# Opening of a decoder-layer kernel: c spread by a VectorE shuffle, squares of four tiles summed on TensorE, the shifted row also kept in float32, and the second block's weights fetched in halves

## The chip, the cores and the metric

The kernel runs on one NeuronCore of a Trainium2 chip. The metric is the device time of one launch in microseconds, as the median of several runs. Engines are named as in the profile: PE is TensorE, DVE is VectorE, ACT is ScalarE, POOL is GpSimd, SP is SyncE, which here only issues DMAs. PEld is PE's loading of weights.

## What is computed

One layer on 256 tokens of width 1024, all in float32: a SwiGLU feed-forward block, a mixer with two branches, and a second SwiGLU block, each behind an RMS norm whose result is scaled and shifted by columns that are computed from a conditioning vector c, and a final norm. The change touches only the beginning of the first SwiGLU block:

```python
c_act = jax.nn.silu(c)
mod = c_act @ ada_w[l] + ada_b[l]
sh1, sc1, g1, sh2, sc2, g2, sh3, sc3, g3 = jnp.split(mod, N_MOD, axis=-1)
u = modulate(rms_norm(h, norm_ffn1_w[l]), sh1, sc1)      # u = normed * (1 + sc1) + sh1
h = h + FFN_RESIDUAL_WEIGHT * g1[:, None, :] * swiglu(u, ffn1_w_in[l], ffn1_w_out[l])
```

## The kernel before

Activations lie transposed: 8 tiles of 128 features by 256 tokens. A float32 product is made of three passes in a faster format (fp32r): each operand is split into a high part (a cast on ACT) and a low part (a subtraction on DVE), and PE multiplies high by high, high by low and low by high.

The opening runs over the eight feature tiles; I call the work of one tile a block and count from 0. For block `kt` the kernel needs a column of the scale (`sc1`), a column of the shift (`sh1`), the normed tile, and 128 rows of `ffn1_w_in` in two parts of 1024 columns (gate and up). Each column is a dot product of 1024 elements in every partition: DVE multiplies 128 rows of `ada_w` (a tile `ada`, its first half for the scale and its second for the shift) by `cb`, the vector silu(c) spread over all partitions, and sums along the row (`ada_dots`, L196). Then:

- ACT makes `am`, the scale with the norm's weight (L416); DVE multiplies the input tile by it and by the reciprocal root of the mean square (`normed`, L425), which gives `xn`.
- ACT makes the shift column `modc` (L420) and then `uh`, the high part of `xn` plus shift (`u_high`, L429). DVE makes `ul`, the low part, from `xn`, the shift and `uh` (`u_low`, L432).
- ACT casts the two halves of the weights to their high parts (`highs`, L410) and DVE makes the low parts (`lows`, L413). Both write to tiles named `wh`.
- PE runs 48 matmuls of 128x256 (`first_mms`, L441): 16 tiles (8 of gate, 8 of up), first high by `uh`, then high by `ul`, then low by `uh`. In the last block the tiles are sorted by pairs, gate and up in turn.

In the opening PE, ACT, DVE and SP work through their instructions in the order in which the code is written (`manual_schedule`): an instruction that waits holds up all that stand behind it on its engine. In the loop over the blocks the code of block `kt + 1` for DVE and ACT stands ahead of the matmuls of block `kt`.

Before block 0, c has to be spread and the statistics made. c is loaded as one row (`crow`, one partition) and spread by two matmuls with a row of ones (L388) into PSUM, from which ACT takes its Silu into `cb` (L185). The tiles of the input come with the identity matrix and a few columns in one tensor, `head`, whose first half is issued on ACT's queue and whose second on SP's. Of each half, ACT squares two tiles and DVE two (L392, L394); DVE adds them (L395, and L397 for the last), and PE sums over partitions by matmuls against a matrix of 1/1024 (`mean1`, L400) into `stat`. ACT takes the root (`r`), DVE the reciprocal, PE spreads it over the partitions (L457), and a few matmuls of ones by ones (`warm`, L377) fill gaps.

All weights are packed by the host in the order in which they are fetched, and `fetch` (L118) issues each as one DMA on SP's queue. For block 0 the gate and up halves are two transfers of 512 KB, for the other blocks one of 1 MB; the scale and shift rows of each block are two of 512 KB. Completions are counted by eight semaphores used in turn, so a DMA is issued only when the one eight before it has landed.

Of the kernel before, what the change touches and what calls it, by code (L numbers as in the profile page):

```python
# [82 lines left out]
def layer(ctx: ExitStack, tc: tile.TileContext, a, out, packing):  # L83
# [14 lines left out]
    def nm(s):  # L98
        uid[0] += 1
        return f"{s}_{uid[0]}"  # L100
# [66 lines left out]
    triu = k[:, K_TRI:K_TRI + P]  # L167
    mean_m = k[:, K_M:K_M + P]
    ones = cst.tile([P, P], F32, name="ones")
    dve.memset(ones, 1.0)  # L170
    epsc = cst.tile([P, 1], F32, name="epsc")
    dve.memset(epsc, EPS)

    phase = {"load": None, "uses": []}

# [178 lines left out]
    with (tc.tile_pool(name="ep", bufs=1) as ep,  # L354
          tc.manual_schedule(engines={e.engine for e in (pe, act, dve, nc.sync)})):
        table("silu_and_others")
        crow = ep.tile([1, D], F32, name="crow")
        nc.sync.dma_start(crow, a["c"])
        for queue, c0, c1 in ((act, 0, 4 * T), (nc.sync, 4 * T, N_HEAD)):
            queue.dma_start(head[:, c0:c1], a["head"][:, c0:c1])  # L360

        def ada01(kt):
            st = ep.tile([P, 2 * D], F32, tag="ada", name=nm("ada"), bufs=4)
            return [ada_rows(st[:, i * D:(i + 1) * D], 1 - i, kt) for i in range(2)]

        def w01(kt):
            st = stage()
            parts = ((0,), (1,)) if kt == 0 else ((0, 1),)
            for js in parts:
                fetch(st[:, js[0] * F1 * P:(js[-1] + 1) * F1 * P], w1, lambda m, js=js: np.stack(  # L370
                    [m[kt * P:(kt + 1) * P, j * FFN:j * FFN + F1 * P] for j in js], axis=1))
            return st.rearrange("p (j n) -> p j n", j=2)

        def warm(n):
            ps = misc_ps()
            for i in range(n):
                pe.matmul(ps[:, :P], ones, ones, start=True, stop=True)  # L377

        sts, wst = [], []
        for kt in range(3):  # L380
            sts.append(ada01(kt))
            wst.append(w01(kt))
# [3 lines left out]
        cps, stat = [misc_ps() for _ in range(2)], misc_ps()  # L386
        for q in range(2):
            pe.matmul(cps[q], ones[0:1, :], crow[:, q * 512:(q + 1) * 512], start=True, stop=True)  # L388
        for i in range(2):
            f0 = 4 * i  # L390
            sq = ep.tile([P, 4, T], F32, tag="sq2", name=nm("sq2"), bufs=2)
            act.activation(sq[:, 0:2, :], h[:, f0:f0 + 2, :], AF.Square)  # L392
            lookup(cb[:, i * 512:(i + 1) * 512], cps[i], AF.Silu)
            dve.tensor_tensor(sq[:, 2:4, :], h[:, f0 + 2:f0 + 4, :], h[:, f0 + 2:f0 + 4, :], ALU.mult)  # L394
            dve.tensor_tensor(sq[:, 0:2, :], sq[:, 0:2, :], sq[:, 2:4, :], ALU.add)  # L395
            if i == 1:
                dve.tensor_tensor(sq[:, 0, :], sq[:, 0, :], sq[:, 1, :], ALU.add)  # L397
            for f in range(2 - i):
                for tt in range(2):
                    pe.matmul(stat[:, tt * P:(tt + 1) * P], sq[:, f, tt * P:(tt + 1) * P], mean1,  # L400
                              start=i == f == tt == 0, stop=i == tt == 1, skip_group_check=True)
        warm(1)
        u = new_u()
        am = sp.tile([P, KD], F32, tag="am", name=nm("am"), bufs=2)

# [21 lines left out]

        def u_high(kt, xn):
            act.activation(u[0][:, kt, :], xn, AF.Identity, bias=modc[:, 0, kt:kt + 1])  # L429

        def u_low(kt, xn):
            dve.scalar_tensor_tensor(u[1][:, kt, :], xn, modc[:, 0, kt:kt + 1],  # L432
                                     u[0][:, kt, :].bitcast(F32), ALU.add, ALU.subtract)

        def first_mms(kt, hw):
            tiles = [(j, f) for j in range(2) for f in range(F1)]
# [2 lines left out]
            for w, x in ((0, 0), (0, 1), (1, 0)):  # L439
                for j, f in tiles:  # L440
# [4 lines left out]
        ada_dots(sts[0][0], 1, 0)  # L445
        dve.scalar_tensor_tensor(bn1, head[:, H_AB + KD:H_AB + 2 * KD], 1.0,
                                 head[:, H_N1:H_N1 + KD], ALU.add, ALU.mult)
        r = ep.tile([P, 2], F32, name="r2")
        table("sqrt_and_others")
        lookup(r, stat[:, 0:T:P], AF.Sqrt, bias=epsc)  # L450
# [8 lines left out]
        warm(3)  # L459
        ada_dots(sts[0][1], 0, 0)  # L460
        xn = normed(0, ps[:, :T])
        shift_col1(0)
# [9 lines left out]
        banks += [[misc_ps().rearrange("p (f t) -> p f t", f=2) for _ in range(2)] for _ in range(2)]  # L472
        for kt in range(KD):
            if kt + 3 < KD:
                sts.append(ada01(kt + 3))
                wst.append(w01(kt + 3))
            if kt + 1 < KD:
                hw_next = halves(kt + 1)
                ada_dots(sts[kt + 1][0], 1, kt + 1)
                scale_col1(kt + 1)  # L480
                highs(kt + 1, hw_next, 0)
                ada_dots(sts[kt + 1][1], 0, kt + 1)
                xn = normed(kt + 1, rb)
                shift_col1(kt + 1)
                u_high(kt + 1, xn)
                highs(kt + 1, hw_next, 1)
                lows(kt + 1, hw_next, 0)
                u_low(kt + 1, xn)
                lows(kt + 1, hw_next, 1)
            first_mms(kt, hw)  # L490
            hw = hw_next
# [626 lines left out]
```

## Time and profile before

| what | value |
|---|---|
| median of 3 runs | 821.73 us (821.46 to 821.89) |
| the profiled execution | 821.32 us |
| its span, from the first to the last instruction | 819.3 us |
| mean granted clock of TensorE | 0.998 |
| first matmul of block 0 (L441) | 11.92 us after the span's start |
| DMA in the first 20 us | 366 GB/s on average |

A row of the timeline gives the start in us from the span's start, the duration, the engine, the line, the operation, what it writes and reads, the shape, how many were merged (x4), and in brackets how long the engine had been idle before and what ended that. Instructions on one engine overlap a little, so the next one's start tells more of the cost than the duration. A row with SPq or ACTq is the issue of a DMA, not the transfer. Matmuls in plain float32 show up as two passes.

### The profile page before, as it was taken

Reading aid. Unit: us, or ns where it says so; the run is one execution under the profiler, and the core shown is the slowest. Engines: PE = TensorE matmul, PEld = TensorE weight load, DVE = VectorE, ACT = ScalarE, POOL = GpSimd, SP = SyncE. Lnnn points to the kernel's source line nnn. Section 1 sums busy time; section 2 is a strip of 40 time slices with the busy share of each in tenths; the row PEclk is TensorE's granted clock in tenths of the full one; section 3 lists DMA queues with packets and bytes.
Section 4 is the critical chain, followed back from the end, with each engine's and each line's share of the span. In section 5 each row is a group of like instructions: output and inputs, shape, how many; then the busy total and the mean of one; then the engine's idle time right before and its main releaser. Section 6 shows DMA issues by size and latency. Waiting matters only on the chain.

```text
span 819.3 us, 15834 instructions
## 1 busy us (share of the span) xinstructions
PE 808.9 (99%) x6580; PEld 782.6 (96%) x6580; DVE 677.3 (83%) x1003; ACT 505.6 (62%) x722; POOL 16.2 (2%) x31
## 2 busy tenths in 40 slices
PE   8999999999999999999999999999999999999997
PEld 6999999999999989999999999999999999999886
DVE  7989899977989889788898778977988987665693
ACT  6565445555898678766465569765658754545342
POOL 0000000000200010000000000000000001100000
PEclk9999999999999999999999999999999999999999
DMA  9999889854695556546658664554565589785521
GB/s 366 414 418 350 312 350 363 341 200 155 233 318 188 202 173 225 189 148 212 239 192 310 231 232 154 206 207 154 193 224 183 198 316 261 277 289 183 194 103 51
DMA packets 31161, 195.69 MB, mean 239 GB/s; under 512 B 3681, under 2 KB 4321, under 8 KB 10482
## 3 DMA queue, kind: packets, MB, share of 16 engines
q1 hardware_dynamic: 28370, 186.07, 62.9%
q0 software_dynamic: 2432, 7.90, 3.1%
q8 instruction: 51, 0.84, 0.4%
q10 hardware_dynamic: 288, 0.72, 0.3%
q14 instruction: 20, 0.16, 0.1%
HBM read 192.54 MB, written 2.13 MB: 238 GB/s over the span
## 4 chain that ended last, share of the span: by engine, by line
PE 93%; DVE 3%; ACT 2%; DMA 1%; issue 0%; SPq 0%; ACTq 0%
PE proj L151 25%; PE proj L153 25%; PE proj L152 25%; PE proj L147 2%; PE proj L148 2%; PE proj L441 2%; PE proj L149 2%; PE misc L441 2%; DMA wst<-in_ffn_w_in_dram 1%; PE misc L746 1%; DVE wh L138 1%; PE misc L890 1%; PE misc L222 1%; PE misc L756 1%; ACT s L185 0%
## 5 line engine op out<-in xcount | busy, mean ns | idle before, releaser
L138 DVE TENSOR_TENSOR wh<-wst,wh 128x1024 fp32r<-128x1024 f32 (+1 forms) x262 | 315.9, 1212 | 85.6 <-ACT wh L137 85.1
L137 ACT CAST wh<-wst 128x1024 fp32r<-128x1024 f32 (+1 forms) x262 | 272.0, 1043 | 164.9 <-PE proj L153 125.0
L151 PE MATMUL proj<-uh,wh 128*128 128x256 f32 (+1 forms) x1096 | 304.0, 277 | 0.0
L152 PE MATMUL proj<-ul,wh 128*128 128x256 f32 (+1 forms) x1096 | 303.1, 277 | 0.0
L153 PE MATMUL proj<-uh,wh 128*128 128x256 f32 (+1 forms) x1096 | 303.0, 276 | 0.0
L153 PEld LDWEIGHTS proj<-uh,wh 128*128 128x128 f32 x1096 | 205.8, 188 | 0.2 <-issue 0.2
L152 PEld LDWEIGHTS proj<-ul,wh 128*128 128x128 f32 x1096 | 205.8, 188 | 0.1
L151 PEld LDWEIGHTS proj<-uh,wh 128*128 128x128 f32 x1096 | 205.8, 188 | 0.1
L151 PE MATMUL proj<-s,wh 128*128 128x256 f32 x312 | 86.7, 278 | 0.2 <-ACT s L142 0.2
L153 PE MATMUL proj<-s,wh 128*128 128x256 f32 x312 | 86.3, 277 | 0.0
L152 PE MATMUL proj<-s,wh 128*128 128x256 f32 x312 | 86.2, 276 | 0.0
L151 PEld LDWEIGHTS proj<-s,wh 128*128 128x128 f32 x312 | 58.5, 188 | 0.4 <-ACT s L142 0.4
L153 PEld LDWEIGHTS proj<-s,wh 128*128 128x128 f32 x312 | 58.6, 188 | 0.0
L152 PEld LDWEIGHTS proj<-s,wh 128*128 128x128 f32 x312 | 58.6, 188 | 0.0
L196 DVE SCALAR_TENSOR_TENSOR ada<-ada,cb 128x1024 f32<-128x1024 f32 x48 | 57.2, 1217 | 0.0
L147 PE MATMUL proj<-uh,wh 128*128 128x256 f32 x152 | 42.0, 276 | 0.0
L148 PE MATMUL proj<-uh,wh 128*128 128x256 f32 x152 | 42.0, 276 | 0.0
L149 PE MATMUL proj<-ul,wh 128*128 128x256 f32 x152 | 42.0, 276 | 0.0
L151 PE MATMUL proj<-ah,wh 128*128 128x256 f32 x152 | 42.0, 276 | 0.0
L152 PE MATMUL proj<-al,wh 128*128 128x256 f32 x152 | 42.0, 276 | 0.0
L153 PE MATMUL proj<-ah,wh 128*128 128x256 f32 x152 | 42.0, 276 | 0.0
L185 ACT ACTIVATE s<-proj 128x512 f32<-128x512 f32 x33 | 19.7, 597 | 35.5 <-PE proj L153 33.4
(271 smaller groups left out, 1371.3 us busy)
## 6 DMA issues: line engine op xcount, KB each, us to landing
wst<-in_mix_w_in_dram SPq DMA_DIRECT2D x52, 1024.0 KB, 4.9
wst<-in_ffn_w_in_dram SPq DMA_DIRECT2D x43, 1024.0 KB, 6.3
wst<-in_ffn_w_out_dram SPq DMA_DIRECT2D x18, 1024.0 KB, 5.0
ada<-in_ada_w_dram SPq DMA_DIRECT2D x16, 1024.0 KB, 8.3
wst<-in_ada_w_dram SPq DMA_DIRECT2D x12, 1024.0 KB, 5.0
ada<-in_ada_w_dram SPq DMA_DIRECT2D x16, 512.0 KB, 12.8
wst<-in_w_br_ssd_dram SPq DMA_DIRECT2D x8, 1024.0 KB, 4.9
wst<-in_w_br_ret_dram SPq DMA_DIRECT2D x8, 1024.0 KB, 4.9
```

The costliest lines, as they stand in the source:

```text
L137: act.copy(hi, v)
L138: dve.tensor_tensor(lo, v, hi.bitcast(F32), ALU.subtract)
L147: pe.matmul(o, l[1], r[0], start=False, stop=False, skip_group_check=skip)
L148: pe.matmul(o, l[0], r[0], start=False, stop=False, skip_group_check=skip)
L149: pe.matmul(o, l[0], r[1], start=False, stop=False, skip_group_check=skip)
L151: pe.matmul(o, l[0], r[0], start=first, stop=False, skip_group_check=skip)
L152: pe.matmul(o, l[0], r[1], start=False, stop=False, skip_group_check=skip)
L153: pe.matmul(o, l[1], r[0], start=False, stop=last, skip_group_check=skip)
L185: phase["uses"].append(act.activation(*args, **kw).ins)
L196: dve.scalar_tensor_tensor(st[:, i, :], st[:, i, :], 1.0, cb, ALU.mult, ALU.mult, accum_out=raw[:, j, f0 + i:f0 + i + 1])
L222: pe.matmul(ps[:, :T], mean, s, start=i == 0, stop=i == len(parts) - 1)
L441: pe.matmul(banks[f // 2][j][:, f % 2, :], hw[w][j][:, f * P:(f + 1) * P], u[x][:, kt, :], start=kt == w == x == f % 2 == 0, stop=kt == KD ...
```

## The change

The constants `ones` and `epsc` are set later. `crow` becomes a tile of 128 partitions that DVE sets to zero; one DMA then writes c into partitions 0, 32, 64 and 96, and a shuffle on DVE copies the first partition of each group of 32 to the whole group, into `cb`. The DMA of c stands behind SP's half of `head` in place of ahead of it, and waits for the zeroing. The Silu is one instruction on `cb` in place of two from PSUM. The matmuls that spread c go; ten matmuls of ones stand in their place, and the other two groups grow from 1 to 2 and from 3 to 5.

For the second half of `head` DVE doesn't add any more: PE sums four squared tiles in place of one.

`u_high` gets a second activation that writes `xn` plus shift, in float32, back to `xn`; `u_low` then subtracts `uh` from it without the shift.

The weights of block 1 are fetched as two halves, in the order scale rows, gate half, shift rows, up half. `block` replaces `ada01` and `w01`; the other blocks' order stays. `bn1` is made ahead of the first dot product.

```diff
-        crow = ep.tile([1, D], F32, name="crow")
-        nc.sync.dma_start(crow, a["c"])
+        crow = ep.tile([P, D], F32, name="crow")
+        dve.memset(crow, 0.0)
+        dve.memset(ones, 1.0)
+        dve.memset(epsc, EPS)
         for queue, c0, c1 in ((act, 0, 4 * T), (nc.sync, 4 * T, N_HEAD)):
             queue.dma_start(head[:, c0:c1], a["head"][:, c0:c1])
+        nc.sync.dma_start(crow[0:P:32, :], a["c"].broadcast_to([4, D]))
...
+            scale = rows(0)
+            if kt == 1:
+                cols(0)
+            shift = rows(1)
+            for js in ((0,), (1,)) if kt == 0 else ((1,),) if kt == 1 else ((0, 1),):
+                cols(*js)
...
-        for q in range(2):
-            pe.matmul(cps[q], ones[0:1, :], crow[:, q * 512:(q + 1) * 512], start=True, stop=True)
+        dve.stream_shuffle(cb, crow, [0] * 32)
+        stat = misc_ps()
+        warm(10)
         for i in range(2):
             f0 = 4 * i
             sq = ep.tile([P, 4, T], F32, tag="sq2", name=nm("sq2"), bufs=2)
             act.activation(sq[:, 0:2, :], h[:, f0:f0 + 2, :], AF.Square)
-            lookup(cb[:, i * 512:(i + 1) * 512], cps[i], AF.Silu)
+            if i == 0:
+                lookup(cb, cb, AF.Silu)
             dve.tensor_tensor(sq[:, 2:4, :], h[:, f0 + 2:f0 + 4, :], h[:, f0 + 2:f0 + 4, :], ALU.mult)
-            dve.tensor_tensor(sq[:, 0:2, :], sq[:, 0:2, :], sq[:, 2:4, :], ALU.add)
-            if i == 1:
-                dve.tensor_tensor(sq[:, 0, :], sq[:, 0, :], sq[:, 1, :], ALU.add)
-            for f in range(2 - i):
+            if i == 0:
+                dve.tensor_tensor(sq[:, 0:2, :], sq[:, 0:2, :], sq[:, 2:4, :], ALU.add)
+            for f in (2, 3, 0, 1) if i else (0, 1):
...
         def u_high(kt, xn):
             act.activation(u[0][:, kt, :], xn, AF.Identity, bias=modc[:, 0, kt:kt + 1])
+            act.activation(xn, xn, AF.Identity, bias=modc[:, 0, kt:kt + 1])

         def u_low(kt, xn):
-            dve.scalar_tensor_tensor(u[1][:, kt, :], xn, modc[:, 0, kt:kt + 1],
-                                     u[0][:, kt, :].bitcast(F32), ALU.add, ALU.subtract)
+            dve.tensor_tensor(u[1][:, kt, :], xn, u[0][:, kt, :].bitcast(F32), ALU.subtract)
```

The order of instructions, first ACT's in one block of the loop (block 1). Before:

```order
L416 ACTIVATE am_143<-raw,bn_116,head 128x1
L410 CAST wh_186<-wst_107 128x1024
L420 ACTIVATE modc<-raw,head 128x1
L429 ACTIVATE uh_141<-xn_192,modc 128x256
L410 CAST wh_187<-wst_107 128x1024
```

After:

```order
L424 ACTIVATE am_157<-raw,bn_118,head 128x1
L418 CAST wh_203<-wst_106 128x1024
L428 ACTIVATE modc<-raw,head 128x1
L437 ACTIVATE uh_155<-xn_209,modc 128x256
L438 ACTIVATE xn_209<-xn_209,modc 128x256
L418 CAST wh_204<-wst_106 128x1024
```

The new activation (L438) stands between `uh` and the second CAST, in each of the eight blocks.

Next DVE's from its start to the reciprocal. Before:

```order
L170 MEMSET ones 128x128
L172 MEMSET epsc 128x1
L384 MEMSET mean_114 128x128
L394 TENSOR_TENSOR sq_10_122<-head 128x512
L395 TENSOR_TENSOR sq_10_122<-sq_10_122 128x512
L394 TENSOR_TENSOR sq_11_131<-head 128x512
L395 TENSOR_TENSOR sq_11_131<-sq_11_131 128x512
L397 TENSOR_TENSOR sq_11_131<-sq_11_131 128x256
L196 SCALAR_TENSOR_TENSOR ada_98,raw<-ada_98,cb 128x1024
L446 SCALAR_TENSOR_TENSOR bn_116<-head 128x8
L454 RECIPROCAL r_146<-r_146 128x2
```

After:

```order
L356 MEMSET crow 128x1024
L357 MEMSET ones 128x128
L358 MEMSET epsc 128x1
L391 MEMSET mean_116 128x128
L393 STREAM_SHUFFLE cb<-crow 128x1024
L402 TENSOR_TENSOR sq_9_132<-head 128x512
L404 TENSOR_TENSOR sq_9_132<-sq_9_132 128x512
L402 TENSOR_TENSOR sq_10_141<-head 128x512
L453 SCALAR_TENSOR_TENSOR bn_118<-head 128x8
L194 SCALAR_TENSOR_TENSOR ada_99,raw<-ada_99,cb 128x1024
L462 RECIPROCAL r_160<-r_160 128x2
```

The shuffle, which waits for the transfer of c, stands ahead of all squares; two adds are gone.

Last SP's first transfers. Before:

```order
L358 DMA crow<-in_c_dram 1x1024
L360 DMA head<-in_head_dram 128x1176
L118 DMA ada_98<-in_ada_w_dram 128x1024 x2
L118 DMA wst_101<-in_ffn_w_in_dram 128x1024 x2
L118 DMA ada_104<-in_ada_w_dram 128x1024 x2
L118 DMA wst_107<-in_ffn_w_in_dram 128x2048
```

After:

```order
L360 DMA head<-in_head_dram 128x1176
L361 DMA crow<-in_c_dram 4x1024
L118 DMA ada_99<-in_ada_w_dram 128x1024 x2
L118 DMA wst_100<-in_ffn_w_in_dram 128x1024 x2
L118 DMA ada_105<-in_ada_w_dram 128x1024
L118 DMA wst_106<-in_ffn_w_in_dram 128x1024
L118 DMA ada_105<-in_ada_w_dram 128x1024
L118 DMA wst_106<-in_ffn_w_in_dram 128x1024
```

c comes second, and block 1's weights (`wst_106`) are two transfers with the shift rows between them.

More of the change, by code (lines that the diff above doesn't have):

```diff
@@ L169, in layer @@
     ones = cst.tile([P, P], F32, name="ones")
-    dve.memset(ones, 1.0)
     epsc = cst.tile([P, 1], F32, name="epsc")
-    dve.memset(epsc, EPS)
     phase = {"load": None, "uses": []}
@@ L356, in layer, with block, rows, cols @@
         table("silu_and_others")
-        crow = ep.tile([1, D], F32, name="crow")
-        nc.sync.dma_start(crow, a["c"])
+        crow = ep.tile([P, D], F32, name="crow")
+        dve.memset(crow, 0.0)
+        dve.memset(ones, 1.0)
+        dve.memset(epsc, EPS)
         for queue, c0, c1 in ((act, 0, 4 * T), (nc.sync, 4 * T, N_HEAD)):
             queue.dma_start(head[:, c0:c1], a["head"][:, c0:c1])
[L362 to L370, printed above, removed]
-                    [m[kt * P:(kt + 1) * P, j * FFN:j * FFN + F1 * P] for j in js], axis=1))
-            return st.rearrange("p (j n) -> p j n", j=2)
+        nc.sync.dma_start(crow[0:P:32, :], a["c"].broadcast_to([4, D]))
+        sts, wst = [], []
+        def block(kt):
+            ada, w = ep.tile([P, 2 * D], F32, tag="ada", name=nm("ada"), bufs=4), stage()
+            def rows(i):
+                return ada_rows(ada[:, i * D:(i + 1) * D], 1 - i, kt)
+            def cols(*js):
+                fetch(w[:, js[0] * F1 * P:(js[-1] + 1) * F1 * P], w1, lambda m: np.stack(
+                    [m[kt * P:(kt + 1) * P, j * FFN:j * FFN + F1 * P] for j in js], axis=1))
+            scale = rows(0)
[4 more added lines that the diff above has]
+                cols(*js)
+            sts.append((scale, shift))
+            wst.append(w.rearrange("p (j n) -> p j n", j=2))
         def warm(n):
@@ L377, in warm @@
                 pe.matmul(ps[:, :P], ones, ones, start=True, stop=True)
-        sts, wst = [], []
         for kt in range(3):
-            sts.append(ada01(kt))
-            wst.append(w01(kt))
+            block(kt)
         mean1 = ep.tile([P, P], F32, name="mean1")
@@ L392, in layer @@
             act.activation(sq[:, 0:2, :], h[:, f0:f0 + 2, :], AF.Square)
[L393 removed]
+            if i == 0:
+                lookup(cb, cb, AF.Silu)
             dve.tensor_tensor(sq[:, 2:4, :], h[:, f0 + 2:f0 + 4, :], h[:, f0 + 2:f0 + 4, :], ALU.mult)
[L395 to L398 removed]
+            if i == 0:
+                dve.tensor_tensor(sq[:, 0:2, :], sq[:, 0:2, :], sq[:, 2:4, :], ALU.add)
+            for f in (2, 3, 0, 1) if i else (0, 1):
                 for tt in range(2):
                     pe.matmul(stat[:, tt * P:(tt + 1) * P], sq[:, f, tt * P:(tt + 1) * P], mean1,
[L401 to L402 removed]
+                              start=i == f == tt == 0, stop=i == f == tt == 1,
+                              skip_group_check=True)
+        warm(2)
         u = new_u()
@@ L458, in layer @@
                       start=True, stop=True)
-        warm(3)
+        warm(5)
         ada_dots(sts[0][1], 0, 0)
@@ L474, in layer @@
             if kt + 3 < KD:
-                sts.append(ada01(kt + 3))
-                wst.append(w01(kt + 3))
+                block(kt + 3)
             if kt + 1 < KD:
```

3 lines of the change are left out of this document (1 added, 2 removed).

## The prediction

> **What bounds the kernel now.** I read the page first: busy time by engine, then the chain of work that ended last.
>
> ```profile
> PE 808.9 (99%) x6580; PEld 782.6 (96%) x6580; DVE 677.3 (83%) x1003; ACT 505.6 (62%) x722; POOL 16.2 (2%) x31
> PE 93%; DVE 3%; ACT 2%; DMA 1%; issue 0%; SPq 0%; ACTq 0%
> ```
>
> PE is busy for 808.9 of 819.3 us and carries 93% of the chain. What the change can win or lose is therefore PE time that is empty, or that it makes empty, in the opening: the eight blocks of L441, 48 matmuls each. Next the chain in order of time, from the span's start:
>
> ```profile
> 4.85 11.54 DMA wst<-in_ffn_w_in_dram
> 16.40 0.40 ACT wh L410
> ...
> 17.68 0.52 ACT uh L429
> 18.24 0.74 PE proj L441 x4
> ```
>
> Block 1's first matmul, at 18.24, hangs on one 1 MB transfer, issued at 4.85 and in use at 16.40. This is the gap that the split fetch is aimed at. From 18.24 on PE has no gap in the opening. The timeline of a later block (block 5), ACT's rows and then DVE's, says why that is a near thing:
>
> ```profile
> 38.18 0.39 ACT L416 ACTIVATE am<-raw,bn,head 128x1 f32<-128x1 f32 x1 [2.44 <-DVE ada L196]
> 38.47 1.04 ACT L410 CAST wh<-wst 128x1024 fp32r<-128x1024 f32 x1
> 39.41 0.28 ACT L420 ACTIVATE modc<-raw,head 128x1 f32<-128x1 f32 x1
> 39.78 0.51 ACT L429 ACTIVATE uh<-xn,modc 128x256 fp32r<-128x256 f32 x1
> 40.20 1.03 ACT L410 CAST wh<-wst 128x1024 fp32r<-128x1024 f32 x1
> ```
>
> ```profile
> 36.91 1.22 DVE L196 SCALAR_TENSOR_TENSOR ada<-ada,cb 128x1024 f32<-128x1024 f32 x1
> ...
> 39.20 0.48 DVE L425 SCALAR_TENSOR_TENSOR xn<-head,am,rb 128x256 f32<-128x256 f32 x1
> 39.60 1.22 DVE L413 TENSOR_TENSOR wh<-wst,wh 128x1024 fp32r<-128x1024 f32 x1
> 40.74 0.48 DVE L432 SCALAR_TENSOR_TENSOR ul<-xn,modc,uh 128x256 fp32r<-128x256 f32 x1
> 41.26 1.23 DVE L413 TENSOR_TENSOR wh<-wst,wh 128x1024 fp32r<-128x1024 f32 x1
> 42.41 1.22 DVE L196 SCALAR_TENSOR_TENSOR ada<-ada,cb 128x1024 f32<-128x1024 f32 x1
> ```
>
> Follow it as a loop between two engines (ACT above, DVE below). DVE makes the dot product with the scale rows (36.91); ACT waits for it, idle for 2.44 us, then does am, the first CAST, the shift column, uh and the second CAST, which ends at 40.20 + 1.03 = 41.23. DVE's second `wh` subtraction starts at 41.26, 0.03 later, though DVE itself was ready sooner: a 128x256 operation lets the next one start 0.40 after it (39.20, 39.60), here at 40.74 + 0.40 = 41.14. The dot product of the next block follows at 42.41. One turn takes 42.41 - 36.91 = 5.50 us and runs **through ACT's second CAST**. PE's turn is hardly longer: from block 1's first matmul at 18.24 to block 7's at 52.05 are six blocks, 5.64 us each.
>
> ```profile
> 52.05 1.18 PE L441 MATMUL proj<-uh,wh 128*128 128x256 f32 x8
> 51.18 1.04 ACT L410 CAST wh<-wst 128x1024 fp32r<-128x1024 f32 x1
> ```
>
> In block 7 the matmuls are sorted so that the third needs the second CAST. That CAST ends at 51.18 + 1.04 = 52.22; PE reaches its third matmul at 52.05 + 2 x 0.12 = 52.29. The slack is 0.07 us.
>
> **The shifted row in float32: the term that decides.** The new `xn` activation (128x256, Identity with a bias) is queued on ACT between uh and the second CAST, so it lies in the loop in every block, eight times. Its form is that of L429. Lower bound: from uh to the next instruction are 40.20 - 39.78 = 0.42 us, as for any instruction that needn't wait. Upper bound: the new one waits on ACT's own semaphore (it overwrites xn, which uh reads), and an instruction that waits so starts 0.09 late: the shift column ends at 39.41 + 0.28 = 39.69 and uh, which reads it, starts at 39.78. That makes 0.51 + 0.09 = 0.60. I take 0.51 us, the row's own duration.
>
> A turn becomes 5.50 + 0.51 = 6.01 us, over PE's 5.64, so PE waits for ACT in each block. Eight of them push the end of the last opening CAST by 8 x 0.51 = **+4.1 us** (3.4 to 4.8). What DVE may save by a plainer `ul` counts nothing: it stands ahead of an instruction that waits for the CAST.
>
> **The second block's weights.** Two waits in the same loop go. Block 1's first CAST stood still until 16.40; by the 0.29 us from am to CAST in block 5 it could have started at 15.24 + 0.29 = 15.53. Block 3's stood 27.52 - 27.05 - 0.29 = 0.18 behind its am. The half now fetched ahead of the shift rows lands one 512 KB transfer sooner, and everything after block 0 is later anyway. Sum: -0.87 - 0.18 = **-1.05 us**. The one DMA more costs SP an issue, beside a queue in which a transfer waited 11.5 us (4.85 to 16.40): nothing.
>
> ```profile
> 15.24 0.39 ACT L416 ACTIVATE am<-raw,bn,head 128x1 f32<-128x1 f32 x1 [0.87 <-DVE ada L196]
> 16.40 1.05 ACT L410 CAST wh<-wst 128x1024 fp32r<-128x1024 f32 x1 [0.78 <-DMA wst<-in_ffn_w_in_dram]
> 27.05 0.39 ACT L416 ACTIVATE am<-raw,bn,head 128x1 f32<-128x1 f32 x1 [2.44 <-DVE ada L196]
> 27.52 1.05 ACT L410 CAST wh<-wst 128x1024 fp32r<-128x1024 f32 x1
> ```
>
> **The start of block 0.** The rows of the opening, in order of time:
>
> ```profile
> 0.74 0.34 SPq L358 DMA_DIRECT2D crow<-in_c_dram  x1
> 0.77 0.38 ACTq L360 DMA_DIRECT2D head<-in_head_dram  x1
> 0.83 0.17 DVE L170 MEMSET ones<- 128x128 f32 x1 [0.83 <-PEq L1077]
> 1.14 0.36 SPq L360 DMA_DIRECT2D head<-in_head_dram  x1
> 4.52 0.69 DVE L394 TENSOR_TENSOR sq<-head 128x512 f32<-128x512 f32 x1 [3.37 <-DMA head<-in_head_dram]
> 5.95 0.69 DVE L394 TENSOR_TENSOR sq<-head 128x512 f32<-128x512 f32 x1
> 9.21 0.26 ACT L185 ACTIVATE r<-misc,epsc 128x2 f32<-128x2 f32 x1 [0.85 <-PE misc L400]
> 9.59 1.21 DVE L196 SCALAR_TENSOR_TENSOR ada<-ada,cb 128x1024 f32<-128x1024 f32 x1
> 11.36 0.51 ACT L429 ACTIVATE uh<-xn,modc 128x256 fp32r<-128x256 f32 x1
> 11.92 0.74 PE L441 MATMUL proj<-uh,wh 128*128 128x256 f32 x4 [0.71 <-ACT uh L429]
> ```
>
> The two halves of head land at 4.5 (ACT's) and 5.95 (SP's); the statistics are done at 9.21, and uh follows 11.36 - 9.21 = 2.15 us later, through the reciprocal, the dot product queued behind it and xn. That tail stays. What moves is 9.21.
>
> c now has to land before anything on DVE: the shuffle is DVE's first instruction that waits, ahead of all squares. Its transfer is issued when the memset of 128x1024 is done (0.83 + 0.06 + 8 x 0.11, scaled from the 128x128 row at 0.17 us of which I put 0.06 down to fixed cost: 1.8) and stands in SP's queue behind SP's head, which is now issued 0.4 sooner, alongside ACT's. Bounds of its landing: 4.7, if SP's head goes first and takes what ACT's took before (3.7 from issue to 4.5) with its greater size; 5.95, if both heads go first. I take the middle, 5.3. The shuffle itself lies between 0.69 (128x512 above) and 1.22 (128x1024, L196); it reads as many elements as the latter, so 1.2. The Trainium skill, "VectorE: DVE Perf Modes", section "The perf-mode tier table", gives about 2400 ns for 2048 elements of a STREAM_SHUFFLE, an estimate of 1.2 us here; the sum would be the same, and no row here shows it.
>
> Then two operations of 0.69 (square, add) and the statistics on PE: 12 matmuls of two passes each in place of 6. A pass took 0.21 us in the first ones and 0.11 later (the first row is the one-row matmuls that spread c):
>
> ```profile
> 2.28 3.75 PE L388 MATMUL misc<-crow,ones 1*128 1x512 f32 x4 [2.28 <-DMA crow<-in_c_dram]
> 6.07 2.47 PE L400 MATMUL misc<-mean,sq 128*128 128x128 f32 x9
> 6.07 3.11 PE L400 MATMUL misc<-mean,sq 128*128 128x128 f32 x12
> 10.37 0.50 PE L377 MATMUL misc<-ones 128*128 128x128 f32 x3
> 10.37 0.83 PE L377 MATMUL misc<-ones 128*128 128x128 f32 x6
> ```
>
> (Three passes more take 0.64, later 0.33.) The ten new warming matmuls start at about 2.0 and last 20 x 0.21 = 4.2 us; the change of speed came under 4 us after the first matmul on 128 rows, at 6.07. So I take 0.11: 24 x 0.11 = 2.7 us. Statistics done: 5.3 + 1.2 + 2 x 0.69 + 0.1 (semaphores) + 2.7 = 10.7, against 9.21: **+1.5 us** (0.9 with c at 4.7, when ACT's head at 5.95 is late; 2.1 with c at 5.95). The two adds taken off DVE are in that count. ACT's one Silu of 1024 elements and its table load run while PE does the statistics; if that cover went, r would wait for the table load.
>
> **Sum.** 4.1 - 1.05 + 1.5 - 0.07 (the slack) = +4.5 us, from bounds of 0.9 + 3.4 - 1.1 = 3.2 to 2.1 + 4.8 - 1.1 = 5.8. The profiled execution took 821.32 us (span 819.3): 825.8. The median of the runs lies 0.4 above it: 826.2. Behind the opening the same instructions follow, with a few of DVE's and ACT's exchanged, under a PE that never waits: nothing comes back there.
>
> **Rivals.**
> *ACT's idle time takes it (not slower).* Were the new activation hidden in the 2.44 us that ACT idles per block, PE would bind again at 5.64 a block, and only the start and block 1's gap, 18.24 - 11.92 - 5.64 = 0.7 us, would count: 821.7 - 0.7 = 821.0 with the start unmoved, 821.0 + 1.5 = 822.5 with it moved as above. It decides from where the second CAST ends before DVE is ready for it; the rows show 41.23 against 41.14, so there is no room even now, and the idle time lies ahead of am, not between uh and the CAST. 8%, and 2% beside it for a gain over 0.2%, which none of these cases reaches.
> *PE is still slow at the statistics.* If the warming matmuls don't bring the fast passes, 24 passes take 24 x 0.10 = 2.4 us more, and half of that if speed changes on the way: 827.4 to 828.6. The 3.75 us of one-row matmuls from 2.28 on brought nothing before, so what counts is uncertain: 22%. The Trainium skill, "TensorE: Matmul & The Clock Gate", Part 1, has the clock doubled after a busy, free-running window of about 3.4 us; 4.2 us of warming mostly fill one, wherever it falls, and by that rule the sum stays; the trace agrees as far as the change some 3.8 us after 6.07 goes.
> *Early landing.* c lands by 3.5 and ACT's head at 4.5 as now; then squares at 4.7 give 4.7 + 1.4 + 0.1 + 2.7 = 8.9, the start is about unmoved, and 4.1 - 1.1 = +3.0 is left, 2.3 at 0.42 an activation: 824.0 to 824.7. 8%.
>
> **How the numbers follow.** The forecast, +4.5, has 60%. Main case, slow PE and early landing are all slower by more than 0.2% (1.6 us, about what a measurement of this kernel can tell from no change): 90%; the same 8%; faster 2%. The range, 823.6 to 828.4, takes in the bounds of the sum, the early landing and most of the slow PE.
>
> **What would show it.** Blocks of about 6.0 us on PE in place of 5.64, each with a wait for the second CAST; that CAST 0.4 to 0.6 later behind uh; `wh` subtractions of DVE that start where it ends. The shuffle starting at c's landing, 4.7 to 5.95; r near 10.7; the first L441 matmul near 13.4. I am wrong if PE's blocks stay at 5.64, if the shuffle starts before 4.5, or if the CAST goes ahead of the new activation.

## The result, and the profile after

| what | before | after |
|---|---|---|
| median of the runs | 821.60 us (821.39 to 821.89, 4 runs) | 828.44 us (827.69 to 830.94, 4 runs) |
| after / before | | 1.0087, 95% interval 1.0074 to 1.0100 |
| the profiled execution, and its span | 821.32, 819.3 us | 829.12, 827.3 us |
| `uh` of block 0 starts | 11.36 us | 15.48 us |
| first matmul behind the opening (L151) | 57.60 us | 65.12 us |
| from there to the end of the span | 761.7 us | 762.2 us |

The change makes the kernel slower, as forecast, but by 6.8 us where 4.5 were predicted: the median lies just above the range. The last rows of the table say where the profiled execution lost it: 7.5 us in the opening, 0.5 behind it. Of the 7.5, 15.48 - 11.36 = 4.1 us are a later start of block 0, and 49.64 - 46.24 = 3.4 us a longer way from there to the first L151.

The page of the changed kernel, its first part (PE) and its chain by engine:

```profile
PE 812.7 (98%) x6614; PEld 787.5 (95%) x6614; DVE 677.7 (82%) x1004; ACT 509.5 (62%) x729; POOL 16.2 (2%) x31
...
PE 88%; DVE 5%; ACT 5%; issue 1%; DMA 0%; ACTq 0%; DVEq 0%
```

PE has lost five points of the chain to DVE and ACT. The waits of PE in the first 66 us of the same kernel (us in total, times, longest) say for what:

```profile
PE proj L449 <- ACT wh L418: 2.7, 8, 1.0
PE misc L407 <- DVE sq L404: 2.1, 1, 2.1
```

The first row is the loop: eight waits for a CAST of the weights, one for each block. Its timeline in block 2, ACT's rows, then DVE's, then PE's:

```profile
25.95 0.39 ACT L424 ACTIVATE am<-raw,bn,head 128x1 f32<-128x1 f32 x1 [2.44 <-DVE ada L194]
26.24 1.04 ACT L418 CAST wh<-wst 128x1024 fp32r<-128x1024 f32 x1
...
27.55 0.52 ACT L437 ACTIVATE uh<-xn,modc 128x256 fp32r<-128x256 f32 x1
28.10 0.51 ACT L438 ACTIVATE xn<-xn,modc 128x256 f32<-128x256 f32 x1
28.52 1.03 ACT L418 CAST wh<-wst 128x1024 fp32r<-128x1024 f32 x1
...
24.69 1.22 DVE L194 SCALAR_TENSOR_TENSOR ada<-ada,cb 128x1024 f32<-128x1024 f32 x1
29.58 1.23 DVE L421 TENSOR_TENSOR wh<-wst,wh 128x1024 fp32r<-128x1024 f32 x1 [0.51 <-ACT wh L418]
...
30.72 1.22 DVE L194 SCALAR_TENSOR_TENSOR ada<-ada,cb 128x1024 f32<-128x1024 f32 x1
...
29.60 0.74 PE L449 MATMUL proj<-uh,wh 128*128 128x256 f32 x4 [0.29 <-ACT wh L418]
```

The second CAST now stands 28.52 - 27.55 = 0.97 us behind uh, where it was 0.42. It ends at 29.55, DVE's subtraction starts at 29.58 after 0.51 us of idling, PE's matmuls that need it at 29.60, and a turn takes 30.72 - 24.69 = 6.03 us in place of 5.50. The 2.44 us that ACT idles ahead of `am` are there to the hundredth as before: nothing of the activation was hidden in them.

The second row of the waits belongs to the start. Its timeline:

```profile
1.96 0.65 SPq L361 DMA_DIRECT2D crow<-in_c_dram  x1
...
2.13 4.54 PE L386 MATMUL misc<-ones 128*128 128x128 f32 x20 [2.13 <-DVE ones L357]
...
6.04 0.63 ACT L399 ACTIVATE sq<-head 128x512 f32<-128x512 f32 x1 [4.02 <-DMA head<-in_head_dram]
...
6.08 1.31 DVE L393 STREAM_SHUFFLE cb<-crow 128x1024 f32<-128x1024 f32 x1
...
7.29 0.66 DVE L402 TENSOR_TENSOR sq<-head 128x512 f32<-128x512 f32 x1
...
8.06 0.69 DVE L404 TENSOR_TENSOR sq<-sq 128x512 f32<-128x512 f32 x1
...
8.80 4.56 PE L407 MATMUL misc<-mean,sq 128*128 128x128 f32 x24 [2.13 <-DVE sq L404]
...
13.40 0.26 ACT L183 ACTIVATE r<-misc,epsc 128x2 f32<-128x2 f32 x1 [3.10 <-PE misc L407]
...
15.48 0.51 ACT L437 ACTIVATE uh<-xn,modc 128x256 fp32r<-128x256 f32 x1 [0.16 <-DVE xn L433]
```

ACT's half of head and c land only at 6.04 and 6.05. The warming matmuls end at 6.67, PE then has nothing for 2.13 us, and the 24 passes of the statistics take 4.56 us, 0.19 each. The windows of 2 us (PE's busy time and matmuls, granted clock, DMA share, GB/s) tell why:

```profile
6.00:8.00 2.00, 0.67 (x4) 1.00 1.02 416
8.00:10.00 2.00, 1.20 (x10) 0.97 1.03 418
10.00:12.00 2.00, 2.00 (x11) 0.50 1.02 408
12.00:14.00 2.00, 1.91 (x12) 0.68 1.03 414
```

Ten passes fit into the 1.20 us before 10.00, eleven into the 2 us behind it: the clock was up when the statistics began, and was halved in the middle of them. It had come up late: the warming's passes go at 0.21 us each, and the trace's clock record has full speed from 6.45 only, 0.2 us before the warming ends.

### The profile page after: what moved, and what is told of

Its sections match the earlier page's. It is cut to its first block, busy times and chain, and to the rows that moved or that the text cites. A ratio compares the mean times of both kernels' runs of the same rounds, so it can differ in the third digit from the quotient of the medians.

```text
span 827.3 us, 15918 instructions
## 1 busy us (share of the span) xinstructions
PE 812.7 (98%) x6614; PEld 787.5 (95%) x6614; DVE 677.7 (82%) x1004; ACT 509.5 (62%) x729; POOL 16.2 (2%) x31
## 3 DMA queue, kind: packets, MB, share of 16 engines
HBM read 192.55 MB, written 2.13 MB: 235 GB/s over the span
## 4 chain that ended last, share of the span: by engine, by line
PE 88%; DVE 5%; ACT 5%; issue 1%; DMA 0%; ACTq 0%; DVEq 0%
PE proj L152 25%; PE proj L151 25%; PE proj L153 25%; PE proj L147 2%; PE proj L148 2%; PE proj L149 2%; ACT wh L418 2%; DVE ada L194 1%; DVE wh L421 1%; PE misc L753 1%; DVE wh L138 1%; PE misc L897 1%; PE misc L407 1%; PE misc L220 1%; PE misc L763 1%
## 5 line engine op out<-in xcount | busy, mean ns | idle before, releaser
L151 PE MATMUL proj<-uh,wh 128*128 128x256 f32 (+1 forms) x1096 | 303.9, 277 | 0.0
L151 PEld LDWEIGHTS proj<-uh,wh 128*128 128x128 f32 x1096 | 205.8, 188 | 0.1
L151 PE MATMUL proj<-s,wh 128*128 128x256 f32 x312 | 86.7, 278 | 0.2 <-ACT s L142 0.2
L151 PEld LDWEIGHTS proj<-s,wh 128*128 128x128 f32 x312 | 58.5, 188 | 0.4 <-ACT s L142 0.4
L151 PE MATMUL proj<-ah,wh 128*128 128x256 f32 x152 | 42.0, 276 | 0.0
```

The source lines that it names most:

```text
L151: pe.matmul(o, l[0], r[0], start=first, stop=False, skip_group_check=skip)
```

## The experiments

The theory after this result has two parts. The activation costs 0.5 us in each of eight turns of the DVE-ACT loop. The start is late because c lands at 6.0 and because PE's clock falls back in the gap between warming and statistics. The rivals: the start alone is the loss and ACT's idle time takes the activation; the 24 passes as such are too many; the landing of c is a matter of its queue.

For reading the runs together, this table has, for the profiled execution of each kernel, the start of `uh` in block 0, the first L151 matmul, the difference, and the rest of the span. All in us.

| kernel | uh, block 0 | first L151 | from uh to L151 | rest |
|---|---|---|---|---|
| before | 11.36 | 57.60 | 46.24 | 761.7 |
| after | 15.48 | 65.12 | 49.64 | 762.2 |
| e1, after without the activation | 16.48 | 62.22 | 45.74 | 762.3 |
| e8, the same with 18 warming matmuls | 13.98 | 59.70 | 45.72 | 762.1 |
| e2, before with the activation | 11.25 | 60.94 | 49.69 | 763.6 |
| e3, after with 18 warming matmuls | 14.11 | 63.74 | 49.63 | 762.4 |
| e10, e3 with a tile of its own | 14.39 | 62.90 | 48.51 | 762.2 |
| e5, e3 with statistics as before | 13.55 | 63.18 | 49.63 | 762.3 |
| e9, e3 with c on GpSimd's queue | 15.44 | 65.14 | 49.70 | 761.7 |
| e6, after with c as before | 14.02 | 63.77 | 49.75 | 762.4 |
| e4, before with block 1 in halves | 11.82 | 57.70 | 45.88 | 762.3 |
| e7, before with blocks 1 to 3 in halves | 12.30 | 57.62 | 45.32 | 763.3 |

The experiments ran on three chips (e1 to e4; e5, e7, e8 and e9; e6 and e10), on which the kernel before took 821.63, 821.54 and 821.45 us. Each ratio is taken on its own chip; where two experiments of different chips are compared, up to 0.2 us can come from that.

**e1, the activation taken out of the changed kernel.** `u_low` adds the shift itself again.

```diff
-            act.activation(xn, xn, AF.Identity, bias=modc[:, 0, kt:kt + 1])
...
-            dve.tensor_tensor(u[1][:, kt, :], xn, u[0][:, kt, :].bitcast(F32), ALU.subtract)
+            dve.scalar_tensor_tensor(u[1][:, kt, :], xn, modc[:, 0, kt:kt + 1],
+                                     u[0][:, kt, :].bitcast(F32), ALU.add, ALU.subtract)
```

> The changed kernel without the second activation; the low part takes the shift itself again. Loop theory (the activation lies in the loop between DVE and ACT and costs 8 x 0.55 us): PE goes back to 5.64 us a block behind an unmoved start near 16.0, so about 4.1 us less, 824.4 us, still 2.8 over the kernel before. Rival (it hides in ACT's idle time, the whole loss comes from the start): no change, 828.4 us, blocks of 6.03 stay.

Measured: 826.38 us (823.98 to 826.67, 4 runs), ratio 1.0049 (1.0034 to 1.0064). That lies midway between the two expectations, and the trace says why it settles neither by its time: the start had moved again. From uh to L151 it has the 45.7 us of the theory, but its statistics ran slowly throughout (the row, and windows as above):

```profile
8.87 5.49 PE L407 MATMUL misc<-mean,sq 128*128 128x128 f32 x24 [2.10 <-DVE sq L404]
...
10.00:12.00 2.00, 2.00 (x11) 1.00 1.03 410
12.00:14.00 2.00, 2.00 (x12) 1.00 1.02 412
```

24 passes at 0.23 us, eleven and twelve in 2 us. This isn't the fall of the result's profile: nothing fell here. The passes are as slow as in the warming and shorten only at about 14.5 (the clock record has 14.52), though the code up to the statistics is the same. In this execution the ten warming matmuls never brought the fast passes. One of its four runs took 823.98 us, near the theory's number. The experiment had to be made again with a start that holds still (e8).

**e2, the activation alone, in the kernel before.** The edit of e1 the other way round.

```diff
             act.activation(u[0][:, kt, :], xn, AF.Identity, bias=modc[:, 0, kt:kt + 1])
+            act.activation(xn, xn, AF.Identity, bias=modc[:, 0, kt:kt + 1])
...
-            dve.scalar_tensor_tensor(u[1][:, kt, :], xn, modc[:, 0, kt:kt + 1],
-                                     u[0][:, kt, :].bitcast(F32), ALU.add, ALU.subtract)
+            dve.tensor_tensor(u[1][:, kt, :], xn, u[0][:, kt, :].bitcast(F32), ALU.subtract)
```

> The kernel before with the second activation alone. Loop theory: blocks of 6.03 us; 8 x 0.55 = 4.4 less the 0.7 that the wait for block 1's weights swallows (ACT stood still there anyway), +3.6 us, 825.2 us. Rival (hidden): 821.6 us, blocks of 5.64.

Measured: 826.65 us (826.14 to 827.12), ratio 1.0060 (1.0043 to 1.0077). The opening is 60.94 - 57.60 = 3.3 us longer, with the same eight waits as in the changed kernel:

```profile
PE proj L441 <- ACT wh L410: 2.8, 8, 1.0
```

So the activation alone makes the loss of the loop, with c, statistics and weights untouched. The other 1.9 us of the profiled run's loss lie behind the opening (the column "rest" above). e7, whose code behind the opening is that of the kernel before as e2's is, has 1.7 more there too, so such differences come without any edit behind the opening; why all four runs of e2 took over 826.1 us stays open.

**e3, eighteen warming matmuls in place of ten.** They end at 8.99, where the statistics begin.

```diff
-        warm(10)
+        warm(18)
```

> The changed kernel with 18 warming matmuls in place of 10, so that PE isn't idle from 6.7 to 8.8 us. Theory of the gap (the granted clock, full from 6.45, falls back at 9.86 because most of the stretch before was idle, and the statistics run at half rate): the clock stays full, the 24 passes of the statistics take about 2.7 us in place of 4.56, r comes near 11.5 in place of 13.40, total 826.5 us, and the runs lie closer together than 827.7 to 830.9. Rival (the statistics are slow for another reason, as their operands or their one PSUM bank): they stay at 4.6 us, total 828.4 us.

Measured: 827.91 us (827.86 to 827.96), ratio 1.0074 (1.0059 to 1.0089).

```profile
9.04 2.94 PE L407 MATMUL misc<-mean,sq 128*128 128x128 f32 x24
...
12.02 0.26 ACT L183 ACTIVATE r<-misc,epsc 128x2 f32<-128x2 f32 x1 [1.48 <-PE misc L407]
...
14.11 0.51 ACT L437 ACTIVATE uh<-xn,modc 128x256 fp32r<-128x256 f32 x1 [0.16 <-DVE xn L433]
```

Without the gap the passes take 0.12 us each, block 0 starts 1.4 us sooner than in the profiled run of the changed kernel, and four runs lie within 0.1 us where the changed kernel's lay 3.3 us apart. So the state of the clock at the statistics is the cause of the spread: the four other kernels with 18 warming matmuls have their runs within 0.2 to 0.6 us too. Whether the closed gap or the longer warm-up does it, e3 can't tell, since it changes both; e9 below has a gap again. The median gains only 0.5 us, less than expected: two of the four runs of the changed kernel took 827.7 us, as if the clock had held in them; no trace of these was taken.

**e8, e1 again on that ground.** The edits of e1 and e3 together.

```diff
-        warm(10)
+        warm(18)
...
-            act.activation(xn, xn, AF.Identity, bias=modc[:, 0, kt:kt + 1])
...
-            dve.tensor_tensor(u[1][:, kt, :], xn, u[0][:, kt, :].bitcast(F32), ALU.subtract)
+            dve.scalar_tensor_tensor(u[1][:, kt, :], xn, modc[:, 0, kt:kt + 1],
+                                     u[0][:, kt, :].bitcast(F32), ALU.add, ALU.subtract)
```

> The changed kernel with 18 warming matmuls in place of 10 (so that the clock holds through the statistics and the runs don't spread) and without the second activation of xn (u_low adds the shift itself, as before). My theory: the activation lies in a loop between ACT and DVE and costs 0.545 us in each block; without it PE's own 5.64 us a block bind again. With the same start as the run with 18 warming matmuls (827.9 us) this gives 823.9 us (4.0 less; 2.2 above the kernel before, all of it the later start less the gap of block 1). Rival, that ACT's 2.4 us of idle time per block hides the activation: 827.9 us, unchanged.

Measured: 823.92 us (823.63 to 824.25, 8 runs), ratio 1.0027 (1.0017 to 1.0038). Against e3's 827.91 the activation costs 4.0 us, with the starts 0.1 us apart. PE's waits for the CAST are gone but for one:

```profile
PE proj L449 <- ACT wh L418: 0.2, 1, 0.2
```

This decides for the loop and against the idle time. It also shows the rest of the change by itself, with 18 warming matmuls in place of ten: 2.4 us slower than the kernel before, on the same chip.

**e10, the activation in a tile of its own.** What of the cost is the instruction, and what the wait for the one ahead of it?

```diff
+        xs = [ep.tile([P, T], F32, name=f"xs{i}") for i in range(2)]
...
-            act.activation(xn, xn, AF.Identity, bias=modc[:, 0, kt:kt + 1])
+            act.activation(xs[kt % 2], xn, AF.Identity, bias=modc[:, 0, kt:kt + 1])
...
-            dve.tensor_tensor(u[1][:, kt, :], xn, u[0][:, kt, :].bitcast(F32), ALU.subtract)
+            dve.tensor_tensor(u[1][:, kt, :], xs[kt % 2], u[0][:, kt, :].bitcast(F32), ALU.subtract)
```

> The changed kernel with 18 warming matmuls, and with the second activation writing to a tile of its own (two in turn) in place of over xn. Theory: the activation costs 0.545 us a block and not the 0.42 of an instruction that needn't wait, because it overwrites what uh reads and so starts only when uh has ended (0.55 behind it). With its own tile it starts 0.42 behind uh, the turn becomes 5.50 + 0.42 = 5.92 us in place of 6.03, and 8 x 0.13 = 1.0 us go: 826.9 us. Rival, that ACT works one instruction after the other and the 0.55 is its own length: 827.9 us, unchanged.

Measured: 826.83 us (826.61 to 826.94), ratio 1.0061 (1.0046 to 1.0076), against e3's 827.91: 1.1 us less, as expected. ACT's rows in one block:

```profile
26.16 0.51 ACT L439 ACTIVATE uh<-xn,modc 128x256 fp32r<-128x256 f32 x1
26.58 0.50 ACT L440 ACTIVATE xs<-xn,modc 128x256 f32<-128x256 f32 x1
26.98 1.03 ACT L418 CAST wh<-wst 128x1024 fp32r<-128x1024 f32 x1
```

The activation now starts 0.42 behind uh in place of 0.55. Writing over `xn` cost 0.13 us in each block: there the activation starts 0.03 us after uh, which reads `xn`, has ended (27.55 + 0.52 = 28.07, 28.10); with its own tile it starts 0.09 before (26.67, 26.58).

**e5, the statistics as before, in the changed kernel with 18 warming matmuls.** DVE adds the squares of the second half again, PE has 12 passes.

```diff
-            if i == 0:
-                dve.tensor_tensor(sq[:, 0:2, :], sq[:, 0:2, :], sq[:, 2:4, :], ALU.add)
-            for f in (2, 3, 0, 1) if i else (0, 1):
+            dve.tensor_tensor(sq[:, 0:2, :], sq[:, 0:2, :], sq[:, 2:4, :], ALU.add)
+            if i == 1:
+                dve.tensor_tensor(sq[:, 0, :], sq[:, 0, :], sq[:, 1, :], ALU.add)
+            for f in range(2 - i):
...
```

> The changed kernel with 18 warming matmuls, and with the squares of the second half added on DVE again (12 passes of PE for the statistics in place of 24). By the rows of the run with 18 warming matmuls: DVE's two adds come back (0.69 + 0.36 us behind the square that ends at 9.58, so the last sum stands at about 10.6), the four passes behind it take 0.5, the root starts at about 11.2 in place of 12.02, but DVE's dot product, then ending at about 11.85, holds the reciprocal: 0.4 us sooner, 827.5 us. If the statistics on PE were a gain in themselves, it would be later than 827.9 by the two adds, about 1 us: 828.9.

Measured: 827.37 us (827.25 to 827.53), ratio 1.0068 (1.0055 to 1.0082), 0.5 less than e3. The rows:

```profile
10.20 0.42 DVE L405 TENSOR_TENSOR sq<-sq 128x256 f32<-128x256 f32 x1
...
10.68 0.71 PE L408 MATMUL misc<-mean,sq 128*128 128x128 f32 x4 [0.69 <-DVE sq L405]
...
11.43 0.26 ACT L183 ACTIVATE r<-misc,epsc 128x2 f32<-128x2 f32 x1 [1.11 <-PE misc L408]
...
11.77 0.16 DVE L462 RECIPROCAL r<-r 128x2 f32<-128x2 f32 x1
```

The root comes 0.6 us sooner than in e3, though DVE does 1.0 us more before it. Even at full speed, twelve more passes on PE cost more here than the two adds that they replace.

**e6, c spread as before, in the changed kernel.** One row, first in SP's queue, matmuls with a row of ones, Silu in two halves from PSUM; no zeroing, no shuffle, no warming ahead of the statistics.

```diff
-        crow = ep.tile([P, D], F32, name="crow")
-        dve.memset(crow, 0.0)
+        crow = ep.tile([1, D], F32, name="crow")
+        nc.sync.dma_start(crow, a["c"])
...
-        nc.sync.dma_start(crow[0:P:32, :], a["c"].broadcast_to([4, D]))
...
-        dve.stream_shuffle(cb, crow, [0] * 32)
-        warm(10)
+        for q in range(2):
+            pe.matmul(cps[q], ones[0:1, :], crow[:, q * 512:(q + 1) * 512], start=True, stop=True)
...
-            if i == 0:
-                lookup(cb, cb, AF.Silu)
+            lookup(cb[:, i * 512:(i + 1) * 512], cps[i], AF.Silu)
```

> The changed kernel with c loaded first, as one row, spread by matmuls with a row of ones and looked up in two halves from PSUM, as in the kernel before; no zeroing, no shuffle, no ten warming matmuls. The statistics stay on PE with 24 passes, the second activation stays. Theory: c's way over DVE is what moves the start; without it the squares start when head lands (4.5 and 5.95 us), PE does the statistics from 6.07 on, half of the passes at 0.21 us and half at 0.11, and uh of block 0 stands at about 12.75 in place of 14.1 (with the clock held) or 15.5: 826.2 us. Rival, that the 24 passes are what is late (they follow the second squares in either case): 827.5 to 828.4 us.

Measured: 827.49 us (826.82 to 827.92), ratio 1.0067 (1.0050 to 1.0084): the rival's number, not mine. Two rows of the timeline:

```profile
3.30 3.75 PE L394 MATMUL misc<-crow,ones 1*128 1x512 f32 x4 [3.30 <-DMA crow<-in_c_dram]
...
6.97 4.93 PE L405 MATMUL misc<-mean,sq 128*128 128x128 f32 x24
```

One of the windows of 2 us of the same kernel (columns as above):

```profile
8.00:10.00 2.00, 2.00 (x11) 1.00 1.04 426
```

c landed 1.0 us later than in the kernel before (3.30 for 2.28), so the statistics began at 6.97; and all 24 passes went at 0.21 us. I had counted on half of them being fast. So c's way over DVE and the doubled statistics don't add up in these runs: either of them alone holds the start near 14 us (e6 14.02, e5 13.55, both together e3 14.11), since with c on PE the passes are slow, and with c on DVE the squares are late. Part of e6's 14.02 is chance: its profiled run is the slowest of its four, and with c in use at 2.28 its statistics could begin at 6.07 in place of 6.97, which puts uh near 13.1 (an estimate), still 1.8 us behind the kernel before. The window has a lesson of its own: eleven passes in 2 us are the slow speed, and the clock column says 1.00. Here and in e1 that column shows nothing of the slow stretch; the passes have to be counted.

**e9, c's transfer on a queue of its own.** GpSimd issues it, behind the same zeroing.

```diff
-        nc.sync.dma_start(crow[0:P:32, :], a["c"].broadcast_to([4, D]))
+        nc.gpsimd.dma_start(crow[0:P:32, :], a["c"].broadcast_to([4, D]))
```

> The changed kernel with 18 warming matmuls, and with c's transfer issued from GpSimd's queue in place of SP's, behind the same zeroing. Theory: c landed at 6.0 to 6.3 us because it stood behind 588 KB of head in the same queue. On a queue of its own it lands by about 4.5, the shuffle is over before head lands at 5.9, the squares start there in place of 7.5, and the start of block 0 comes 1.2 us sooner: 826.7 us. Rival, that the transfer is late because the engines that move data are full with both halves of head: c lands at 5.5 to 6.3 as before, 827.4 to 827.9 us.

Measured: 828.66 us (828.58 to 828.78), ratio 1.0084 (1.0070 to 1.0098): slower than e3 by 0.75, outside both expectations. Timeline:

```profile
1.18 0.89 SPq L118 DMA_DIRECT2D ada<-in_ada_w_dram  x2
...
2.13 6.42 PE L386 MATMUL misc<-ones 128*128 128x128 f32 x36 [2.13 <-DVE ones L357]
2.24 0.74 POOL L361 DMA_DIRECT2D crow<-in_c_dram  x1 [1.80 <-DVE mean L391]
...
7.60 0.01 DVE L393 LOAD_MASK_SELECT cb<-crow  x1 [5.38 <-DMA crow<-in_c_dram]
...
10.38 2.94 PE L407 MATMUL misc<-mean,sq 128*128 128x128 f32 x24 [1.83 <-DVE sq L404]
```

c lands at 7.60, 5.4 us after its issue. As SP no longer waits for the zeroing, it sends the `ada` rows at 1.18 in place of 2.67, and they are in flight ahead of c. My theory, that a queue of its own lets c land by 4.5, falls. A reading that fits is the rival carried further: the engines that move data are full, and c lands when about what was issued ahead of it, on whatever queue, has been moved. It isn't shown: GpSimd's queue is of another kind in the DMA view (software_dynamic, SP's is hardware_dynamic), and no run has c on it without the `ada` rows ahead, so that queue's own delay isn't told apart. Block 0 starts 1.3 us later than in e3, as the shuffle does (7.63 for 6.33). The rest of the span is 0.7 shorter than e3's in the profiled runs, within what the table shows of scatter.

The last row says something of the clock too. Between the warming, which ends at 8.55, and the statistics PE is idle for 1.83 us, not much less than the 2.13 of the changed kernel; yet the 24 passes take 2.94 us as in e3, and the four runs lie within 0.2 us. Behind 18 matmuls such a gap did no harm, so the gap by itself isn't the whole cause.

**e4, block 1's weights in halves, in the kernel before.** The order scale rows, gate half, shift rows, up half for block 1, nothing else.

```diff
+            scale = rows(0)
+            if kt in (1,):
+                cols(0)
+            shift = rows(1)
+            for js in ((0,), (1,)) if kt == 0 else ((1,),) if kt in (1,) else ((0, 1),):
+                cols(*js)
...
```

> The kernel before with block 1's weights in two halves as in the change, and nothing else. My step (both waits go, but PE's own pace of 5.64 and the weights of blocks 2 and 3 bind next): block 1 starts at 17.55 in place of 18.24, but block 3 still waits for its weights near 27.5, so the total moves by -0.1 us, 821.5. Rival (block 1's gap is worth its 0.7 us to the end): 820.9 us.

Measured: 821.97 us (821.76 to 822.56, 10 runs), ratio 1.0005 (0.9995 to 1.0014), no difference that can be measured. Block 1's wait goes. Block 2's first CAST, which didn't wait before, now waits for its 1 MB, and block 3's waits longer than before (0.64 us behind its am for 0.47):

```profile
21.79 1.05 ACT L416 CAST wh<-wst 128x1024 fp32r<-128x1024 f32 x1 [0.21 <-DMA wst<-in_ffn_w_in_dram]
...
27.60 1.05 ACT L416 CAST wh<-wst 128x1024 fp32r<-128x1024 f32 x1 [0.26 <-DMA wst<-in_ffn_w_in_dram]
```

From uh to L151 the profiled run is 0.36 us shorter than the kernel before, but its c landed 0.8 us later (3.10 for 2.28) and block 0 started 0.5 us later, so a gain of that size can't be told from the scatter of the start.

**e7, blocks 1, 2 and 3 in halves, in the kernel before.** This was the try to beat both kernels; the lines are against e4.

```diff
-            if kt in (1,):
+            if kt in (1, 2, 3):
                 cols(0)
...
-            for js in ((0,), (1,)) if kt == 0 else ((1,),) if kt in (1,) else ((0, 1),):
+            for js in ((0,), (1,)) if kt == 0 else ((1,),) if kt in (1, 2, 3) else ((0, 1),):
```

> The kernel before, with the weights of blocks 1, 2 and 3 fetched in halves (scale rows, gate half, shift rows, up half) in place of block 1 alone; nothing else of the change. Theory: fetching block 1 alone in halves gained nothing, since block 3's first CAST then waited for its 1 MB; with three blocks in halves none of the eight blocks waits for a transfer, and PE's 5.64 us a block bind from block 0 on: 0.7 us less than before, 820.9 us. Rival, that the landing of the halves only moves the wait from the gate half to the up half: 821.6 us, unchanged.

Measured: 822.02 us (821.29 to 823.17, 11 runs), ratio 1.0006 (0.9997 to 1.0015). Inside the opening the theory holds: 45.32 us from uh to L151, eight times PE's 5.64 and a little, the shortest of all runs. But in the profiled run uh came 0.9 us later, behind a c that landed at 3.43, and the end of the opening is where it was (57.62). Whether it gains when c lands early is not told apart by these runs; a gain, if there is one, is below what they resolve.

## Why the prediction was right or wrong

**The bound and the loop: right.** The turn was forecast at 6.01 us through ACT's second CAST and is 6.03; PE waits for that CAST once in each block; ACT's idle time hides nothing (e8 against e3: 4.0 us for the forecast 4.1). The cost of the activation was taken as 0.51 where uh to CAST grew by 0.55: the upper bound's reason, the wait for the engine's own instruction, was the true one (e10), though the start came 0.03 us after the end of uh and not 0.09, and 8 x 0.04 = 0.3 us were missing. That 4.0 lies so near 4.1 is in part luck: eight turns of 0.55 more are 4.4, and in e8 PE too is held at the last CAST (the wait of 0.2 above).

**The weights: right in the sum, not by the split.** I counted -1.05 us for the two waits, and the way from uh to L151 came out at 3.4 us longer for 4.1 - 1.05 - 0.07 = 3.0. But e2, with the weights fetched as before, has the same 49.7 us there: the slower loop alone makes block 1 and block 3 late enough, all but 0.1 us in block 1 (am at 15.68, CAST at 16.07). With the activation the split adds nothing that shows; in the kernel before it moves the wait to blocks 2 and 3 (e4).

**The start of block 0: wrong in size, and this is the step that failed.** Forecast +1.5 (0.9 to 2.1), measured +4.1 in the profiled run and +2.75 with the clock held (e3). Link by link, in the profiled run: c landed at 6.05 for 5.3, just beyond the end of my bounds (+0.75); from there to the first square 1.24 for 1.2, and to the statistics 1.51 for 1.48, as worked out; the 24 passes took 4.56 for 2.7 (+1.9); and the rest to uh 2.08 for 2.15. That is the whole difference of 2.6 us. So two terms were mis-sized: the landing of c, and the passes taken at 0.11 us each. With the clock held, in e3, the first is still there (c in use at 6.30, +1.0) and the second nearly gone (2.94 for 2.7).

For c's landing the upper bound's case came true, and I had taken the middle. I let SP's head take ACT's old place and c slip in behind it. With both heads issued 0.03 us apart, ACT's half lands at 6.04, where the later half of before did (5.95), and c, behind SP's half, with it.

**The clock at the statistics: the rival with 22% was the case, in one run as stated and in the other by a mechanism that I hadn't named.** The rival was that the warming doesn't bring the fast passes. That is what e1's profiled run shows, whose code up to the statistics is that of the changed kernel: slow passes throughout, and uh at 16.48 for 14.11 in e3, 2.4 us. In the changed kernel's own profiled run the warming did bring them, but late, and the granted clock was halved again in the middle of the statistics: 1.4 us. I asked whether the warming would raise the speed; I didn't ask how late it may, nor whether it would stay. The numbers for the second stood in the prediction: warming from about 2.0 for 4.2 us, statistics from 5.3 + 1.2 + 1.4 + 0.1 = 8.0 on. That is a gap of 1.8 us on PE, which became 2.13. The two runs at 827.7 us suggest a third case, in which the clock held, at no price: hence the spread. The run at 830.94 us, 3.0 above e3, left no trace, and what it met stays open.

Eighteen matmuls cure all of this, but the runs don't say by which of their two effects. In the five kernels that have them the passes shorten between 5.5 and 7.6 us from the span's start, well before the warming ends, and e9 keeps them through a gap of 1.83 us. In the changed kernel the clock fell 3.4 us after it had risen (6.45 to 9.86), and of these PE was busy for 1.3 (0.2 before the gap and 1.1 behind it); in e9, of the 3.4 us behind the rise, for 1.9. So how full that stretch is may be what counts; that is a guess from two runs. The Trainium skill, "TensorE: Matmul & The Clock Gate", Part 1, gives the half rate after at least one idle window of about 3.4 us, and windows that run freely; by that a gap of 2.1 us would have been safe. Here it wasn't; the run-to-run spread agrees with freely running windows.

**Behind the opening: right.** 0.5 us in the profiled run, within what the kernels above, edited in the opening alone, show there (761.7 to 763.6).

**Sum.** In the profiled runs 2.6 us of the miss are the start, 0.4 the loop and 0.5 the rest of the span; less 0.2 around the span that makes 829.12 - 825.8 = 3.3. The median of the runs lies 2.2 above the forecast; the two that suggest a held clock (827.7) lie 1.5 above it, within the stated range.

## What to carry to other kernels

Before an instruction is added to an engine that is idle half of the time, follow the loop between the engines: an instruction between a producer and the one that others wait for costs its full length in each turn, and something more if it overwrites what its neighbour reads. When a warm-up is to raise TensorE's clock for some work, make it long enough for the latest rise that the traces show (ten matmuls were at the edge), count the idle time between the two, and let the warm-up run into that work. A small transfer that an engine's whole queue waits for belongs ahead of the large ones: here it landed between 2.3 and 3.4 us when it was issued first, and at 6.0 to 7.6 behind them, and a queue of its own didn't help.

## What the runs showed of the hardware

- Ten warming matmuls (20 passes, 4.5 to 4.6 us from 2.13 on) were at the edge. In one profiled run the passes shortened from 0.21 to 0.11 us from 6.45 on, and after a gap of 2.13 us on PE the granted clock fell to 0.50, about 1.1 us after PE was busy again; in another (e1) they stayed at 0.21 until about 14.5. The changed kernel's runs spread over 3.3 us.
- With eighteen the passes shortened between 5.5 and 7.6 in five profiled runs and stayed short, in e9 through a gap of 1.83 us; the runs of each kernel lie within 0.1 to 0.6 us.
- The column of the granted clock stands at 1.00 while the first passes go at half speed (e6 and e1: eleven passes in 2 us). It shows the later fall to 0.50 and the return.
- Four rows of 4 KB, issued behind two halves of head, landed 4.1 us after their issue on the same queue (1.96 to 6.05) and 5.4 us after it on GpSimd's queue, with 1 MB of `ada` rows ahead of them as well (2.24 to 7.60).
- c as one row, issued first at 0.74 us, was in use at 2.28, 2.53, 3.10, 3.30 and 3.43 us in five kernels that issue it alike.
- Between two activations of 128x256 on ACT lie 0.42 us where the second is free, and 0.55 where it overwrites the input of the first.
- A shuffle of 128x1024 in float32 took 1.31 us, a memset of that size 0.91.
